# A gated-attention encoder layer: the residual x reaches the output projection by accumulating DMAs instead of plain loads

## The chip, the cores and the metric

The kernel runs on one core of a Trainium2 chip. The metric is the device time of one execution in microseconds (us), taken as the median of several runs. The profile shows one execution of the kernel before. Engines: PE is TensorE (PEld its weight load), DVE is VectorE, ACT is ScalarE, POOL is GpSimd, SP is SyncE, which only issues transfers.

## What is computed

One encoder layer on x of 1024 rows by 1024 columns. Two branches (gated linear attention, and windowed pooling) are projected and merged; what matters here is the end:

```python
DEEPNORM_ALPHA = (2.0 * DEPTH) ** 0.25          # DEPTH = 1
merged = g_a * (y_a @ w_proj_a) + g_b * (y_b @ w_proj_b)
y = merged @ w_out
return _layernorm(DEEPNORM_ALPHA * x + y, ln_g, ln_b)

def _layernorm(x, g, b):
    mu = jnp.mean(x32, axis=-1, keepdims=True)
    var = jnp.mean(jnp.square(x32 - mu), axis=-1, keepdims=True)
    return ((x32 - mu) * lax.rsqrt(var + EPS) * g + b).astype(x.dtype)
```

A layer norm does not change when its input and the root of its eps are both multiplied by one constant. So the norm of alpha·x + y with eps is the norm of x + y/alpha with eps/alpha².

## The kernel before

**Products.** A matrix product is done in blocks of two by two quarters, with seven block products in place of eight (`PRODUCTS`, called 1 to 7). Each is twelve matmuls of 128x128 by 128x512: four steps of k, each three times, since every operand is split into a high and a low part (`split`: ACT casts the high part, DVE subtracts it to get the low one). The weights of a product are the operands B11, B21, B22 and T1 to T4 (sums and differences of quarters), made by `Operands.make` in 128x1024 pieces; the rows' side is made by `prep` (DVE sums `raw…`) and `ring_split` (`whi`, `wlo`).

**The w_out stage.** Four objects `Pair` (o0 to o3, from `out_pair`) each give two row blocks of 128: pair tb gives rows tb and tb+4. Their products are interleaved for o0 and o1, then come o2 and o3. Each pair has PSUM banks by tag: `a` (products 1, 2), `c` (7, 4), `b` (6, with T2) and `d` (5, 3); a tag has two buffers (`bank`). Sums common to several quarters, `u` and `e`, are made from banks a, b, c.

**The residual.** `residual` allocates a row `z` and loads x into it on SP's queue (eight loads of 512 KB). `pre` then makes alpha·z + u (or e) on DVE, and `use` adds the product's bank. The first quarter, (0,0), is alpha·z + bank a.

**The norm.** For o0 to o2: after each half row ACT sums it (`junk_…s`, with tb, i, half in its name, written to a spare PSUM buffer of tags b and d in turn); after the fourth, `norm_pair` takes the mean (`nm`), ACT squares four half rows into spare PSUM buffers, DVE and POOL (a power) make the factor, `shifted` scales the row on ACT and multiplies by ln_g on DVE, and POOL issues an accumulating DMA that adds the row to `out`, where ln_b has been stored. For the last pair, o3, `bn_stats` and `norm_one` on DVE do it, and SP stores half rows.

**Order.** The program's order gives the priorities; a scheduler with its own timing then fixes the sequence of each engine. Each engine runs its instructions in that sequence, so an instruction that waits holds up all that stand behind it. In both kernels the end of PE's sequence is: o2's T2, o2's T1, o3's B11, o2's T4 and B22, o3's T3, B21, T2, T1, T4, B22 (twelve matmuls each, the B11 of o3 partly before T4).

Of the kernel before, what the change touches and what calls it, by code (L numbers as in the profile page):

```python
# [7 lines left out]
F32 = mybir.dt.float32  # L8
# [3 lines left out]
AF = mybir.ActivationFunctionType  # L12
ALU = mybir.AluOpType
# [3 lines left out]
P = 128  # L17
S = 1024
D = 1024
# [9 lines left out]
EPS = 1e-5  # L29
AHEAD = 3  # L30
LEAD = 4
ALPHA = 2.0 ** 0.25
# [4 lines left out]
def encoder_layer(ctx: ExitStack, tc: tile.TileContext, xT, x, w_av, w_v, w_blk, w_up, b_al, g_norm,  # L37
                  w_pool, p_scale, b_mrg, w_pa, w_pb, w_o, ln_g, ln_b, ident_c, rcnt_c, masks_c, out):
    nc = tc.nc
    act, dve, pool_e, pe, sp = nc.scalar, nc.vector, nc.gpsimd, nc.tensor, nc.sync  # L40
# [10 lines left out]
    def split(src, hi, lo, lo_eng=None):  # L51
        act.copy(hi, src)  # L52
        (lo_eng or dve).tensor_tensor(out=lo, in0=src, in1=hi.bitcast(F32), op=ALU.subtract)  # L53
# [129 lines left out]
    def at(q):  # L183
        return int(q[0]) - 1, int(q[1]) - 1

    class Operands:
        def __init__(self, nm, fetch):
            self.nm, self.fetch, self.ops, self.pool, self.td = nm, fetch, {}, {}, {}

        def ahead(self, g, piece, eng):  # L190

            q = {}
            for n in ("22", "12", "11", "21"):
                q[n] = piece(n, f"{self.nm}p{n}_{g}")
                self.fetch(q[n], n, g)
            for o, out_, a, b, op in (("T3", "22", "22", "12", ALU.subtract), ("T1", "12", "12", "11", ALU.subtract),
                                      ("T2", "11", "22", "11", ALU.add), ("T4", "21", "21", "11", ALU.subtract)):
                eng.tensor_tensor(out=q[out_], in0=q[a], in1=q[b], op=op)
                self.td[o, g] = dram.tile([P, 2, 512], F32, name=f"{self.nm}{o}_{g}d", tag=f"{self.nm}{o}_{g}d")
                sp.dma_start(self.td[o, g], q[out_])  # L200

        def make(self, o, pool):

            self.pool[o] = pool
            self.ops[o] = [pool.tile([P, 4, 512], F32R, tag="op", name=f"{self.nm}{o}{n}") for n in "hl"]
            for g in range(2):
                t = c4.tile([P, 2, 512], F32, tag="c", name=f"{self.nm}{o}_{g}")
                with tc.high_priority(offset=120):
                    if o[0] == "T":
                        sp.dma_start(t, self.td[o, g])  # L210
                    else:
                        self.fetch(t, o[1:], g)
                split(t, *(x[:, 2 * g:2 * g + 2, :] for x in self.ops[o]))

    X = Operands("x", lambda t, q, g: sp.dma_start(
        t, xT.rearrange("(k p) t -> p k t", p=P)[:, 4 * at(q)[0] + 2 * g:4 * at(q)[0] + 2 * g + 2, at(q)[1] * 512:at(q)[1] * 512 + 512]))
    WO = Operands("wo", lambda t, q, g: sp.dma_start(
        t, w_o[at(q)[1], 4 * at(q)[0] + 2 * g:4 * at(q)[0] + 2 * g + 2].rearrange("k p c -> p k c")))
    for q in ("11", "21", "22"):
        X.ops["B" + q] = [xq[n][at(q)[0]][at(q)[1]] for n in range(2)]  # L220
        X.pool["B" + q] = op_a
# [21 lines left out]
    for half in range(2):  # L243
        ps = ps_m.tile([P, 512], F32, tag="m", name=f"ps_at{half}")
# [204 lines left out]
            dve.tensor_copy(v[b][:, hs], po)  # L449
            act.activation(po, v[b][:, hs], AF.Square, accum_out=d["ss"][:, b:b + 1])  # L450

    def rsqrt_mean(ss, n, pool, nm, w, meanwhile=lambda: None):

        a = pool.tile([P, w], F32, tag="rs_a", name=f"rsa_{nm}", bufs=2)
        r = pool.tile([P, w], F32, tag="rs_r", name=f"rsr_{nm}", bufs=2)
        t = pool.tile([P, w], F32, tag="rs_t", name=f"rst_{nm}", bufs=2)
        dve.tensor_scalar(out=a, in0=ss, scalar1=1.0 / n, scalar2=EPS, op0=ALU.mult, op1=ALU.add)
        pool_e.tensor_tensor(out=r, in0=a, in1=mhalf[:, :w], op=ALU.pow)  # L458
        meanwhile()
        dve.tensor_tensor(out=t, in0=r, in1=r, op=ALU.mult)  # L460
        dve.tensor_tensor(out=t, in0=t, in1=a, op=ALU.mult)
        dve.tensor_scalar(out=t, in0=t, scalar1=-0.5, scalar2=1.5, op0=ALU.mult, op1=ALU.add)
        dve.tensor_tensor(out=r, in0=r, in1=t, op=ALU.mult)
        return r
# [115 lines left out]
    post = ctx.enter_context(tc.tile_pool(name="post", bufs=1, reuse_waits="tile"))  # L580
# [3 lines left out]
    hs_ = (slice(0, 512), slice(512, 1024))  # L584

    def row(nm):
        return c4.tile([P, S], F32, tag="c", name=nm)
# [209 lines left out]
    for gi in (0, 1, 3, 2):  # L797
        pair, p = pool_pair(gi)
# [17 lines left out]
    more = [ahead(YB, 0), None, ahead(YB, 1), None]  # L816
# [9 lines left out]
    more = [ahead(YA, 0), ahead(YA, 1), None, change(X, YB)]  # L826
# [51 lines left out]
    ln, z, st = {}, {}, {}  # L878
# [6 lines left out]

    def residual(tb):
        z[tb] = row(f"z_{tb}")
        with tc.high_priority(offset=150):
            sp.dma_start(z[tb], x[tb * P:tb * P + P, :])

# [7 lines left out]
    def small(nm, shape, tag, bufs=2):  # L898
        return post.tile([P] + shape, F32, tag=tag, name=nm, bufs=bufs)

    def shifted(t, r, nb):

        act.activation(z[t], z[t], AF.Identity, bias=nb, scale=r)
        for i in range(2):
            dve.tensor_tensor(out=z[t][:, hs_[i]], in0=z[t][:, hs_[i]], in1=ln["g"][i], op=ALU.mult)
        pool_e.dma_start(out[t * P:t * P + P, :], z[t], accum_op=ALU.add)

    def norm_pair(tb, sm):

        ln_rows()  # L910
        nm, ss = small(f"nm_{tb}", [2], "nm"), small(f"ss_{tb}", [2, 2], "ssq")
        dve.tensor_tensor(out=nm, in0=sm[:, :, 0], in1=sm[:, :, 1], op=ALU.add)
        for i in range(2):
            for half in range(2):
                junk = bank(f"junk_{tb}{i}{half}", next(spare))
                act.activation(junk, z[tb + 4 * i][:, hs_[half]], AF.Square, bias=nm[:, i:i + 1], accum_out=ss[:, i, half:half + 1])
        s2 = small(f"s2_{tb}", [2], "s2")
        dve.tensor_tensor(out=s2, in0=ss[:, :, 0], in1=ss[:, :, 1], op=ALU.add)
        r = rsqrt_mean(s2, D, post, f"ln{tb}", 2)
        nb = small(f"nb_{tb}", [2], "nb")  # L920
        dve.tensor_tensor(out=nb, in0=nm, in1=r, op=ALU.mult)
        for i in range(2):
            shifted(tb + 4 * i, r[:, i:i + 1], nb[:, i:i + 1])

    def norm_one(t, st):
        mv = small(f"mv_{t}", [2], "mv")
        dve.bn_aggr(out=mv, in_=st)
        zz = z[t]
        r = rsqrt_mean(mv[:, 1:2], 1, post, f"ln{t}", 1, meanwhile=lambda: [
            dve.scalar_tensor_tensor(out=zz[:, cs], in0=zz[:, cs], scalar=mv[:, 0:1], in1=ln["g"][i],  # L930
                                     op0=ALU.subtract, op1=ALU.mult) for i, cs in enumerate(hs_)])
        for i, cs in enumerate(hs_):
            dve.scalar_tensor_tensor(out=zz[:, cs], in0=zz[:, cs], scalar=r, in1=ln["b"][i], op0=ALU.mult, op1=ALU.add)
            sp.dma_start(out[t * P:t * P + P, cs], zz[:, cs])

    def out_pair(tb):
        end = tb == 3
        sm, st = [], {}

        def fetch(t, i, h):  # L940
            t = k4(t)
            if h == 0 or tb > 1:
                sp.dma_start(t, m_d[h][:, :, cols(tb, i)])
            else:
                for k in range(4):
                    dve.tensor_copy(t[:, k, :], m_last[4 + k][:, cols(tb, i)])

        def part(i, half):
            t = tb + 4 * i
            if t not in z:  # L950
                residual(t)
            return z[t][:, hs_[half]]

        def pre(i, half, more):
            o = part(i, half)
            dve.scalar_tensor_tensor(out=o, in0=o, scalar=ALPHA, in1=more, op0=ALU.mult, op1=ALU.add)

        def use(i, half, ps, more):
            o = part(i, half)
            if more is None:  # L960
                dve.scalar_tensor_tensor(out=o, in0=o, scalar=ALPHA, in1=ps, op0=ALU.mult, op1=ALU.add)
            else:
                dve.tensor_tensor(out=o, in0=ps, in1=o, op=ALU.add)
            if end:
                if i not in st:
                    st[i] = small(f"bst_{tb}{i}", [2, 6], "bst")
                dve.bn_stats(out=st[i][:, half, :], in_=o)
                if (i, half) == (1, 0):
                    norm_one(tb + 4, st[1])
            else:  # L970
                if not sm:
                    sm.append(small(f"sm_{tb}", [2, 2], "sm"))
                junk = bank(f"junk_{tb}{i}{half}s", next(spare))
                act.activation(junk, o, AF.Identity, scale=-1.0 / D, accum_out=sm[0][:, i, half:half + 1])

        def done():
            if end:
                norm_one(tb, st[0])
            else:
                norm_pair(tb, sm[0])  # L980

        return Pair(f"o{tb}", fetch, WO, use, done, late={"22": 1} if tb < 2 else None, pre=pre, order="1765423" if end else "1765243")

    outs = [out_pair(tb) for tb in range(4)]
    n = len(items) - 10
# [73 lines left out]
```

## Time and profile before

| | |
|---|---|
| median of 3 runs | 953.77 us (953.29 to 954.65) |
| the profiled execution | 952.35 us, span of the trace 950.6 us |
| mean granted clock of PE | 0.992 of full speed |
| busy share of the span | PE 97%, DVE 78%, ACT 42%, POOL 5% |
| w_out's products in the trace | about 849 us to 941 us; the rest of the span, 9.7 us, is the last norm |

The table says how full each engine is over the whole; the change touches only the last 100 us or so, and those are read in the rows further down.

### The profile page before, as it was taken

How to read it: one execution, taken by the hardware profiler on the slowest of the kernel's cores; microseconds unless marked ns; L12 is line 12 of the kernel's file. 1: busy time of each engine (PE TensorE's matmuls, PEld its weight loads, DVE VectorE, ACT ScalarE, POOL GpSimd, SP SyncE). 2: the span in 40 equal slices, each digit the busy share in tenths (PEclk: the TensorE clock that was granted, in tenths of full speed). 3: DMA queues.
4: the chain of work that ended last, by engine and by line, in shares of the span. 5: the costliest groups of instructions: out<-in, count | busy, mean ns of one | idle time of the engine just before them, and what ended most of it. 6: DMA issues, size and time to landing. Idle time of an engine off the chain costs nothing. (4 is left out here: it accounts for less than half of the span.)

```text
span 950.6 us, 13001 instructions
## 1 busy us (share of the span) xinstructions
PE 926.2 (97%) x4744; PEld 752.7 (79%) x4744; DVE 738.3 (78%) x1168; ACT 401.5 (42%) x676; POOL 43.0 (5%) x35
## 2 busy tenths in 40 slices
PE   9999999999999999999999999999999999997995
PEld 6887897987888887888878778888888878775873
DVE  5448969879768658868787788787787977799777
ACT  5156335354241326323333333346552533644661
POOL 1430000000010000000000000000000000000021
PEclk9999999999999999999999999999999999998998
DMA  8931112323316666162222289798696786769264
GB/s 270 362 115 35 59 57 58 95 73 86 114 51 206 220 198 242 65 249 92 69 75 70 90 309 356 242 365 294 210 344 198 271 292 211 232 204 354 63 128 93
DMA packets 84143, 169.13 MB, mean 178 GB/s; under 512 B 11456, under 2 KB 28096, under 8 KB 84080
## 3 DMA queue, kind: packets, MB, share of 16 engines
q1 hardware_dynamic: 83216, 165.16, 51.0%
q0 software_dynamic: 864, 3.15, 2.0%
q8 instruction: 37, 0.61, 0.3%
q14 instruction: 26, 0.21, 0.1%
HBM read 114.80 MB, written 53.48 MB: 177 GB/s over the span
## 5 line engine op out<-in xcount | busy, mean ns | idle before, releaser
L123 PE MATMUL ps_la<-xh,whi_la 128*128 128x512 f32 x128 | 51.6, 403 | 0.0
L123 PE MATMUL ps_la<-xl,whi_la 128*128 128x512 f32 x128 | 51.4, 402 | 0.0
L123 PE MATMUL ps_la<-xh,wlo_la 128*128 128x512 f32 x128 | 50.9, 398 | 0.0
L52 ACT CAST whi_gb<-raw_gb 128x512 fp32r<-128x512 f32 x28 | 17.3, 621 | 48.8 <-PE psd_pi L638 14.8
L141 PE MATMUL ps_v<-whi_v,xh 128*128 128x264 f32 x128 | 37.2, 292 | 0.2 <-DVE v L150 0.2
L141 PE MATMUL ps_v<-wlo_v,xh 128*128 128x264 f32 x128 | 37.2, 292 | 0.0
L141 PE MATMUL ps_v<-whi_v,xl 128*128 128x264 f32 x128 | 36.5, 286 | 0.0
L52 ACT CAST whi_lb<-raw_lb 128x512 fp32r<-128x512 f32 x28 | 17.4, 621 | 36.9 <-PE psd_lb L638 9.1
L52 ACT CAST whi_pi<-raw_pi 128x512 fp32r<-128x512 f32 x28 | 17.4, 620 | 32.8 <-PE psd_gb L638 7.1
L52 ACT CAST whi_gta<-raw_gta 128x512 fp32r<-128x512 f32 x28 | 17.3, 618 | 32.4 <-DVE raw_gta L623 7.3
L52 ACT CAST whi_pb<-raw_pb 128x512 fp32r<-128x512 f32 x28 | 17.1, 619 | 32.7 <-PE psd_pb L638 11.2
L458 POOL TENSOR_TENSOR rsr_ln<-rsa_ln,mhalf 128x2 f32<-128x2 f32 (+1 forms) x5 | 4.6, 924 | 581.0 <-PE psc_o L638 569.1
L123 PEld LDWEIGHTS ps_la<-xh,wlo_la 128*128 128x128 f32 x128 | 24.1, 188 | 5.7 <-issue 0.4
L123 PEld LDWEIGHTS ps_la<-xh,whi_la 128*128 128x128 f32 x128 | 24.1, 188 | 5.4
L123 PEld LDWEIGHTS ps_la<-xl,whi_la 128*128 128x128 f32 x128 | 24.1, 188 | 5.3
L389 ACT ACTIVATE e<-e 128x1024 f32<-128x1024 f32 x20 | 21.0, 1058 | 17.1 <-DVE e L388 17.1
L449 DVE COPY v<-ps_o 128x256 f32<-128x256 f32 x32 | 13.5, 423 | 18.4 <-PE ps_o L446 11.3
L52 ACT CAST whi_o<-raw_o 128x512 fp32r<-128x512 f32 x28 | 16.9, 616 | 24.6 <-DVE raw_o L623 8.8
L53 DVE TENSOR_TENSOR wlo_pi<-raw_pi,whi_pi 128x512 fp32r<-128x512 f32 x28 | 19.2, 686 | 10.3 <-ACT whi_pi L52 10.0
L450 ACT ACTIVATE ps_o<-v 128x256 f32<-128x256 f32 x32 | 12.4, 388 | 32.6 <-DVE v L449 32.6
L392 DVE TENSOR_TENSOR qs<-q,e 128x1024 f32<-128x1024 f32 x20 | 24.3, 1214 | 2.3 <-ACT e L389 1.5
L123 PE MATMUL ps_k<-xh,whi_k 128*128 128x512 f32 x64 | 25.8, 402 | 0.0
(586 smaller groups left out, 3043.5 us busy)
## 6 DMA issues: line engine op xcount, KB each, us to landing
raw_v<-in_w_v SPq DMA_DIRECT2D x16, 264.0 KB, 2.6
xp<-in_xT SPq DMA_DIRECT2D x8, 512.0 KB, 6.6
oT<-oTs SPq DMA_DIRECT2D x32, 128.0 KB, 2.6
raw_la<-in_w_blk SPq DMA_DIRECT2D x8, 512.0 KB, 3.4
wop<-in_w_o SPq DMA_DIRECT2D x8, 512.0 KB, 4.6
la<-la SPq DMA_DIRECT2D x8, 512.0 KB, 3.1
raw_pi<-in_w_blk SPq DMA_DIRECT2D x16, 256.0 KB, 4.1
raw_gb<-in_w_blk SPq DMA_DIRECT2D x16, 256.0 KB, 2.7
```

The lines of the kernel that those rows point to most:

```text
L52: act.copy(hi, src)
L53: (lo_eng or dve).tensor_tensor(out=lo, in0=src, in1=hi.bitcast(F32), op=ALU.subtract)
L123: pe.matmul(ps[:, half * 512:half * 512 + 512], lhsT=a, rhs=mov(b, k, half), start=(i == 0), stop=(i == 23))
L141: pe.matmul(o, lhsT=sta(a, k, tb), rhs=w(k - k0)[b], start=(k == 0 and i == 0), stop=(k == KB - 1 and i == 2))
L389: act.activation(e, e, AF.Exp, scale=1.0 / TAU)
L392: dve.tensor_tensor(out=qs, in0=qt[h], in1=e, op=ALU.mult)
L449: dve.tensor_copy(v[b][:, hs], po)
L450: act.activation(po, v[b][:, hs], AF.Square, accum_out=d["ss"][:, b:b + 1])
L458: pool_e.tensor_tensor(out=r, in0=a, in1=mhalf[:, :w], op=ALU.pow)
```

## The change

Four things change. First, the rows of o0, o1 and o2 are no longer loaded: `use` writes the product's bank plus u or e to the half row of z (ACT copies bank a for the first quarter, DVE adds for the others), and then POOL issues a DMA that adds 256 KB of x to that half row in SBUF: twelve such DMAs; six loads of 512 KB leave SP's queue, two (for o3) stay. `pre` is left for o3 alone. Second, 1/alpha goes into w_out's operands as they are made (`act.mul` in place of the cast, a scalar_tensor_tensor in place of the subtraction) and 1/alpha² into eps, so that z is x + y/alpha. Third, `shifted` scales in two halves. Fourth, through these the scheduler orders the engines anew.

```diff
     class Operands:
-        def __init__(self, nm, fetch):
+        def __init__(self, nm, fetch, scale=None):
+            self.scale = scale
...
-                split(t, *(x[:, 2 * g:2 * g + 2, :] for x in self.ops[o]))
+                hi, lo = (x[:, 2 * g:2 * g + 2, :] for x in self.ops[o])
+                if self.scale is None:
+                    split(t, hi, lo)
+                else:
+                    act.mul(hi, t, self.scale)
+                    dve.scalar_tensor_tensor(out=lo, in0=t, scalar=self.scale, in1=hi.bitcast(F32), op0=ALU.mult, op1=ALU.subtract)
...
     def residual(tb):
         z[tb] = row(f"z_{tb}")
+        if tb % 4 < 3:
+            return
         with tc.high_priority(offset=150):
             sp.dma_start(z[tb], x[tb * P:tb * P + P, :])
...
     def shifted(t, r, nb):
-        act.activation(z[t], z[t], AF.Identity, bias=nb, scale=r)
         for i in range(2):
+            act.activation(z[t][:, hs_[i]], z[t][:, hs_[i]], AF.Identity, bias=nb, scale=r)
             dve.tensor_tensor(out=z[t][:, hs_[i]], in0=z[t][:, hs_[i]], in1=ln["g"][i], op=ALU.mult)
...
-        r = rsqrt_mean(s2, D, post, f"ln{tb}", 2)
+        r = rsqrt_mean(s2, D, post, f"ln{tb}", 2, EPS / ALPHA ** 2)
...
         def pre(i, half, more):
             o = part(i, half)
-            dve.scalar_tensor_tensor(out=o, in0=o, scalar=ALPHA, in1=more, op0=ALU.mult, op1=ALU.add)
+            dve.tensor_tensor(out=o, in0=o, in1=more, op=ALU.add)
 
         def use(i, half, ps, more):
             o = part(i, half)
-            if more is None:
-                dve.scalar_tensor_tensor(out=o, in0=o, scalar=ALPHA, in1=ps, op0=ALU.mult, op1=ALU.add)
+            if end:
+                dve.tensor_tensor(out=o, in0=ps, in1=o, op=ALU.add)
             else:
-                dve.tensor_tensor(out=o, in0=ps, in1=o, op=ALU.add)
+                if more is None:
+                    act.copy(o, ps)
+                else:
+                    dve.tensor_tensor(out=o, in0=ps, in1=more, op=ALU.add)
+                t = tb + 4 * i
+                pool_e.dma_start(o, x[t * P:t * P + P, hs_[half]], accum_op=ALU.add)
...
-        return Pair(f"o{tb}", fetch, WO, use, done, late={"22": 1} if tb < 2 else None, pre=pre, order="1765243" if ...)
+        return Pair(f"o{tb}", fetch, WO, use, done, late={"22": 1} if tb < 2 else None, pre=pre if end else None, order=...)
```

Three places of the new order follow. In the names, `whi_6_o0` is the high part for product 6 of pair o0, `z_4` is row block 4.

**Start of w_out, ACT.** ACT's sequence where the last pieces of operand B21 are made and the products with T2 (product 6 of o0 and o1) get ready. Before:

```order
L52 CAST woB21h_7397<-woB21_0_7399 128x1024
L52 CAST woB21h_7397<-woB21_1_7403 128x1024
L52 CAST woT4h_7456<-woT4_0_7458 128x1024
L52 CAST whi_6_o0_7557<-raw11_o0_7306 128x512
L52 CAST woT4h_7456<-woT4_1_7462 128x1024
L52 CAST whi_6_o1_7582<-raw11_o1_7344 128x512
```

ACT's sequence at the same place after the change:

```order
L218 ACTIVATE woB21h_7397<-woB21_0_7399 128x1024
L218 ACTIVATE woB21h_7397<-woB21_1_7403 128x1024
L52 CAST whi_6_o0_7557<-raw11_o0_7306 128x512
L218 ACTIVATE woT4h_7456<-woT4_0_7458 128x1024
L52 CAST whi_6_o1_7582<-raw11_o1_7344 128x512
L52 CAST whi_5_o0_7600<-raw21_o0_7370 128x512
```

The cast for product 6 of o0 now stands ahead of the first piece of T4. On DVE, the four sums `raw…` that these casts read stood behind the second piece of `woB21l`, and now stand ahead of it.

**Middle of w_out, ACT.** ACT's sequence around the operand of product 2 of o2. Before:

```order
L974 ACTIVATE junk_110s_7798,sm_1_7713<-z_5_7665 128x512
L916 ACTIVATE junk_000_7831,ss_0_7829<-z_0_7642,nm_0_7828 128x512
L52 CAST whi_2_o2_7936<-raw12_o2_7779 128x512
L643 COPY u_o2_7932<-psa_o2_7919 128x512
L916 ACTIVATE junk_010_7835,ss_0_7829<-z_4_7638,nm_0_7828 128x512
```

And ACT's sequence there after the change, from the sum over the last half row of o0:

```order
L987 ACTIVATE junk_001s_7815,sm_0_7678<-z_0_7724 128x512
L924 ACTIVATE junk_000_7828,ss_0_7826<-z_0_7724,nm_0_7825 128x512
L924 ACTIVATE junk_001_7830,ss_0_7826<-z_0_7724,nm_0_7825 128x512
L924 ACTIVATE junk_010_7832,ss_0_7826<-z_4_7675,nm_0_7825 128x512
L924 ACTIVATE junk_011_7834,ss_0_7826<-z_4_7675,nm_0_7825 128x512
L52 CAST whi_2_o2_7938<-raw12_o2_7774 128x512
L649 COPY u_o2_7934<-psa_o2_7921 128x512
```

The cast `whi_2_o2` now stands behind that sum, which waits for the accumulating DMA of the half row, and behind all four squares of o0.

**End of w_out, POOL.** POOL's whole sequence from the norm of o0 to the last row that it adds to `out`. Before:

```order
L906 DMA out_0<-z_0_7642 128x1024
L906 DMA out_0<-z_4_7638 128x1024
L906 DMA out_0<-z_1_7669 128x1024
L906 DMA out_0<-z_5_7665 128x1024
L458 TENSOR_TENSOR rsr_ln2_8079<-rsa_ln2_8078,mhalf_82 128x2
L906 DMA out_0<-z_2_7979 128x1024
L906 DMA out_0<-z_6_7975 128x1024
```

POOL's sequence there after the change (`z_2` and `z_6` are the rows of o2):

```order
L914 DMA out_0<-z_0_7724 128x1024
L976 DMA z_2_8017<-in_x 128x512
L914 DMA out_0<-z_4_7675 128x1024
L976 DMA z_6_7995<-in_x 128x512 x2
L914 DMA out_0<-z_1_7748 128x1024
L914 DMA out_0<-z_5_7700 128x1024
L976 DMA z_2_8017<-in_x 128x512
L464 TENSOR_TENSOR rsr_ln2_8080<-rsa_ln2_8079,mhalf_82 128x2
L914 DMA out_0<-z_2_8017 128x1024
```

The four half rows of o2 are interleaved with the four rows of o0 and o1 that go out, and the last half row stands behind all four. On DVE at the end, the two multiplications by ln_g of row z_6 and the two L938 of row z_7 stood ahead of the last add (`z_3` with bank d) before, and stand behind it now.

## Rows read from the trace of the kernel before

**Rows 1.** The page, busy time, share and instructions of each engine.

```profile
PE 926.2 (97%) x4744; PEld 752.7 (79%) x4744; DVE 738.3 (78%) x1168; ACT 401.5 (42%) x676; POOL 43.0 (5%) x35
```

**Rows 2.** Windows of 20 us: busy time and count by engine, granted clock, DMA share, GB/s.

```profile
860.00:880.00 20.00, 13.77 (x53) 10.62 (x53) 17.98 (x27) 9.52 (x13) 0.00 (x0) 0.83 0.97 364
880.00:900.00 20.00, 20.00 (x88) 16.24 (x87) 14.43 (x25) 11.06 (x28) 0.00 (x0) 1.00 0.24 69
```

**Rows 3.** Timeline of PE: start, duration, what, idle time before and its releaser.

```profile
866.05 0.80 PE L638 MATMUL psb_o<-woT2h,whi_o 128*128 128x512 f32 x1 [5.98 <-ACT whi_o L52]
...
907.07 0.40 PE L638 MATMUL psd_o<-woT1h,whi_o 128*128 128x512 f32 x1
907.30 0.40 PE L638 MATMUL psd_o<-woT1l,whi_o 128*128 128x512 f32 x1
...
922.48 0.50 PE L638 MATMUL psa_o<-woB21h,whi_o 128*128 128x512 f32 x1 [1.30 <-ACT whi_o L52]
...
924.55 0.63 PE L638 MATMUL psa_o<-woB21h,wlo_o 128*128 128x512 f32 x1
924.98 0.63 PE L638 MATMUL psa_o<-woB21h,whi_o 128*128 128x512 f32 x1
...
927.54 0.50 PE L638 MATMUL psb_o<-woT2h,whi_o 128*128 128x512 f32 x1
...
937.66 0.47 PE L638 MATMUL psd_o<-woB22h,whi_o 128*128 128x512 f32 x1 [1.48 <-DVE z L963]
...
940.30 0.40 PE L638 MATMUL psd_o<-woB22h,wlo_o 128*128 128x512 f32 x1
```

**Rows 4.** Timeline of ACT, 861 to 866 us.

```profile
861.85 1.04 ACT L52 CAST woB21h<-woB 128x1024 fp32r<-128x1024 f32 x1 [2.51 <-DMA woB<-in_w_o]
864.43 1.04 ACT L52 CAST woT4h<-woT 128x1024 fp32r<-128x1024 f32 x1 [1.54 <-DMA woT<-woT_0d]
865.38 0.61 ACT L52 CAST whi_o<-raw_o 128x512 fp32r<-128x512 f32 x1
```

**Rows 5.** Timeline of DVE, 862 to 867 us.

```profile
862.92 1.22 DVE L53 TENSOR_TENSOR woB21l<-woB,woB21h 128x1024 fp32r<-128x1024 f32 x1 [2.02 <-ACT woB21h L52]
864.07 2.49 DVE L623 TENSOR_TENSOR raw_o<-raw_o,raw_o 128x512 f32<-128x512 f32 x4
```

**Rows 6.** DMA issues, 850 to 951 us: count, KB each, median us to landing.

```profile
out<-z SPq DMA_DIRECT2D x4, 256.0 KB, 2.0
```

**Rows 7.** Timeline of POOL, 919 to 934 us: issues of accumulating rows.

```profile
919.87 0.86 POOL L906 DMA_DIRECT2D out<-z  x1 [6.13 <-ACT junk_210s L974]
921.66 0.86 POOL L906 DMA_DIRECT2D out<-z  x1 [0.94 <-ACT whi_o L52]
...
933.08 0.90 POOL L906 DMA_DIRECT2D out<-z  x1 [5.91 <-DVE z L905]
```

**Rows 8.** Landings of POOL's rows: those issued at 919.87 and 921.66, then at 933.08.

```profile
DMA to landing us min/median/max: 6.8/7.2/7.5
...
DMA to landing us min/median/max: 5.3/5.3/5.3
```

**Rows 9.** Window holding the last two accumulating rows, columns as in rows 2.

```profile
933.00:943.00 10.00, 6.23 (x26) 4.36 (x24) 9.87 (x24) 0.00 (x0) 2.95 (x4) 1.00 0.65 105
```

**Rows 10.** The page's DMA queues: packets, MB, share of 16 engines over the span.

```profile
q1 hardware_dynamic: 83216, 165.16, 51.0%
q0 software_dynamic: 864, 3.15, 2.0%
```

**Rows 11.** Groups by form, 870 to 951 us: busy us, mean ns, idle before.

```profile
L916 ACT ACTIVATE junk<-z,nm 128x512 f32<-128x512 f32 x12 | 8.1, 677 | 0.6 <-DVE nm L912 0.6
L905 DVE TENSOR_TENSOR z<-z,lng 128x512 f32<-128x512 f32 x12 | 7.7, 687 | 0.7 <-ACT z L903 0.7
```

**Rows 12.** Timeline of DVE at the end.

```profile
939.51 1.40 DVE L930 SCALAR_TENSOR_TENSOR z<-z,mv,lng 128x512 f32<-128x512 f32 x2
...
940.91 0.68 DVE L963 TENSOR_TENSOR z<-psd_o,z 128x512 f32<-128x512 f32 x1
```

More of the change, by code (lines that the diff above doesn't have):

```diff
@@ L217, in encoder_layer @@
     WO = Operands("wo", lambda t, q, g: sp.dma_start(
-        t, w_o[at(q)[1], 4 * at(q)[0] + 2 * g:4 * at(q)[0] + 2 * g + 2].rearrange("k p c -> p k c")))
+        t, w_o[at(q)[1], 4 * at(q)[0] + 2 * g:4 * at(q)[0] + 2 * g + 2].rearrange("k p c -> p k c")), 1.0 / ALPHA)
     for q in ("11", "21", "22"):
@@ L450, in outputs, with rsqrt_mean @@
             act.activation(po, v[b][:, hs], AF.Square, accum_out=d["ss"][:, b:b + 1])
-    def rsqrt_mean(ss, n, pool, nm, w, meanwhile=lambda: None):
+    def rsqrt_mean(ss, n, pool, nm, w, eps=EPS, meanwhile=lambda: None):
         a = pool.tile([P, w], F32, tag="rs_a", name=f"rsa_{nm}", bufs=2)
@@ L456, in rsqrt_mean @@
         t = pool.tile([P, w], F32, tag="rs_t", name=f"rst_{nm}", bufs=2)
-        dve.tensor_scalar(out=a, in0=ss, scalar1=1.0 / n, scalar2=EPS, op0=ALU.mult, op1=ALU.add)
+        dve.tensor_scalar(out=a, in0=ss, scalar1=1.0 / n, scalar2=eps, op0=ALU.mult, op1=ALU.add)
         pool_e.tensor_tensor(out=r, in0=a, in1=mhalf[:, :w], op=ALU.pow)
@@ L928, in norm_one @@
         zz = z[t]
-        r = rsqrt_mean(mv[:, 1:2], 1, post, f"ln{t}", 1, meanwhile=lambda: [
+        r = rsqrt_mean(mv[:, 1:2], 1, post, f"ln{t}", 1, EPS / ALPHA ** 2, meanwhile=lambda: [
             dve.scalar_tensor_tensor(out=zz[:, cs], in0=zz[:, cs], scalar=mv[:, 0:1], in1=ln["g"][i],
@@ L980, in done @@
                 norm_pair(tb, sm[0])
-        return Pair(f"o{tb}", fetch, WO, use, done, late={"22": 1} if tb < 2 else None, pre=pre, order="1765423" if end else "1765243")
+        return Pair(f"o{tb}", fetch, WO, use, done, late={"22": 1} if tb < 2 else None, pre=pre if end else None, order="1765423" if end else "1765243")
     outs = [out_pair(tb) for tb in range(4)]
```

## The prediction

> **What bounds the kernel now.** I read the page first: PE is busy 97% of the span [rows 1], so a change can only win where PE waits, and DVE passes that vanish while PE runs are worth nothing. The windows show where PE waits in w_out's stage. From 860 to 880 us it is busy 13.77 of 20, at a mean granted clock of 0.83 and with the DMA engines at 0.97; from 880 to 900 it is full while DVE is busy 14.43 of 20 [rows 2]. PE's timeline then gives every wait that matters: 5.98 us before the first T2 product, which waits for ACT's cast `whi`; 1.30 before o3's B21; 1.48 before the last product, where a PSUM bank waits for DVE's add; 940.7 is where PE ends [rows 3]. Matmuls follow each other 0.23 us apart at full clock (907.07 to 907.30) and 0.43 apart after a wait, while the clock is at its lower level (924.55 to 924.98) [rows 3]. So twelve matmuls are 2.8 us, and the dozen after a long wait costs up to some 2 us more.
>
> The whole forecast therefore has five terms: four PE waits that shrink, appear or move, and the tail after the last matmul.
>
> **a) The first wait, 5.98 us.** Now: ACT's second half of `woB21h` ends at 862.89, then ACT waits for the T4 piece until 864.43, casts it, and only then, at 865.38, makes `whi` for product 6 [rows 4]. DVE meanwhile makes `woB21l` from 862.92 and the four sums from 864.07 [rows 5]. After the change the sums stand ahead of `woB21l` and the cast stands right behind `woB21h`: it starts at about 862.9 instead of 865.38, so PE starts 2.5 us earlier. Bounds: 3.5 if the loads of B21 and T4 also land earlier, now that four 512 KB loads of x no longer stand beside them; 0.5 if they land later, since B21's last load stands two transfers further back on SP. **−2.5.**
>
> The other small edits cost nothing here: the scaled cast and the scaled subtraction take the places of passes of the same size on the same engines, and the nine DVE passes of `pre` that vanish lie in stretches where PE is full [rows 2]. Scaling in half rows adds six ACT instructions off the path; the loads that leave SP are only felt in a).
>
> **What an accumulating half row costs.** No row of before has x added to SBUF. The nearest are POOL's six rows into `out`, 512 KB each. They hold the 16 DMA engines 2.0% of 950.6 us [rows 10], which is 19 us, or 3.2 us each; the only two in 933 to 943 us say the same, 0.65 of 10 us [rows 9]. One that starts on an empty queue lands 5.3 us after issue [rows 7, 8], so about 2.1 us are fixed. Two issued 1.8 us apart, at 919.87 and 921.66, landed after 6.8 and 7.5 us [rows 7, 8], so 2.5 us apart: they pass one behind the other on POOL's queue. I take 3.0 for a row when rows queue (bounds 2.5 and 3.25). For a half row the lower bound is a plain transfer of 256 KB, by SP's queue 0.51 x 950.6 us for 165.16 MB [rows 10], 0.77 us; the upper is a whole row, 3.25, if the count of packets and not the bytes sets the time. I take half a row, 1.5, and 2.1 fixed behind it.
>
> The Trainium skill, page "DMA: Bandwidth & Descriptors", section "Anatomy of one DMA — SWDGE (gpsimd) path", fits a transfer issued from GpSimd as about 2.0 us plus its bytes over 436 KB per us. By that a whole row would land in 3.2 us and a half row in 2.6; the trace's 5.3 disagrees for rows that accumulate, though the fixed part agrees.
>
> **b) A new wait before o2's product 2.** PE runs o0's last product, o1's, o2's B11 and T3, then o2's B21. From the end of o0's last product that leaves 36 matmuls, 8.4 us. ACT's cast for B21 now stands behind the sum of o0's last half row and four squares. So after that product come: the add, 0.7 (a DVE pass of 128x512, 0.69 [rows 11]); the half row, 2.1 + 1.5; the sum, 0.8; small steps, 0.3; four squares of 0.7 (0.677 and the gap [rows 11]), 2.8; the cast, 0.6 [rows 4]. That is 8.8, plus about 1 because the half row of o1 before it is still on the queue: 9.8, 1.4 late. Bounds 0.4 (plain rate) and 2.6 (whole-row price). **+1.4.**
>
> **c) The wait before o3's T2.** This is the largest term. T2 of o3 writes bank `b`, and that buffer is held by a square of o2 (`junk_200`), which needs o2's mean, which needs the sum of o2's last half row, `junk_201s`, which now waits for the landing of POOL's last half row. On POOL's queue that transfer stands behind four rows of `out` and three half rows. Before, from the end of o2's T2 (907.07) to o3's T2 (927.54) took 20.5 us [rows 3], for 72 matmuls that need 16.7 (the rest are waits at 922.48 and the lower clock behind them).
>
> After: the first of the rows goes out once its last multiplication is done, which on DVE stands right behind `u`, two passes or 1.35 us after T2's end. Then the queue must pass four rows (4 x 3.0), four half rows (4 x 1.5) and, on the same DMA engines, the two loads that remain for o3 (2 x 1.54 by SP's rate [rows 10]): 21.1. The fixed part is 2.1. Then sum, mean and one square, 0.8 + 0.2 + 0.9 = 1.9. Together 26.5, against 20.5: **+6.0.** Bounds with rows at 2.5 and half rows at 0.77: +1.0; with rows at 3.25 and half rows at 1.6: +7.4.
>
> A check from the other side: POOL issues two of these rows shortly ahead of the last half row. Were nothing else queued, it would still land 2 x 3.0 + 1.5 + 2.1 = 9.6 us after issue, and PE has only T3 and B21, 5.6 us, less the add and 1.9.
>
> **d) From o3's T2 to PE's end.** 13.2 us now (927.54 to 940.7), with the 1.48 wait [rows 3]. That wait goes, since two multiplications by ln_g and a `pre` no longer stand ahead of the add on DVE. But after a wait of 6 us or more the clock falls, as it did for the eight matmuls behind the first wait, which is 8 x 0.2 = 1.6, or 1.7 with the start. **+0.2**, bounds −1.5 and +2.
>
> **e) The tail.** 9.7 us from PE's end to the span's end, DVE busy throughout. Two L930 (1.40 together) lie just ahead of the last add, at 939.51, and the add at 940.91 [rows 12]; they and two multiplications by ln_g of 0.69 [rows 11] now stand behind it. That is 2.6, less about 0.5 that covers waits for POOL's powers: **+2.1**, bounds 1.3 and 2.6. Cover gone, it is the 2.6.
>
> **Sum.** −2.5 + 1.4 + 6.0 + 0.2 + 2.1 = +7.2. The profiled execution took 952.35 us, so 959.55; the median of the runs is 1.42 above it (953.77), which gives **961.0 us**. The five bounds added up give −2.3 and +14.1 (951.5 to 967.9), the likeliest case's own range.
>
> **Rivals.** A measurement of this kernel tells 0.2%, 1.9 us, from no change: 951.9 and 955.7 are the borders.
>
> *B, half rows are cheap and quick: faster.* If a half row lands like SP's plain store of 256 KB, 2.0 us after issue [rows 6], and does not stand behind the rows for `out`, T2 of o3 finds its bank free. From the end of o2's last product to o3's T2 there are 24 matmuls, 5.6 us; less the add (0.7) and 1.9, a landing within 3.0 us means no wait at all. Then c) is 16.7 − 20.5 = −3.8, d) −1.5, b) 0.4, a) and e) as above: −5.3, or 948.5. It decides from a landing of about 8 us downward, where c) is +1.5 and the sum zero. Against it: rows do queue [rows 8], and one alone took 5.3. The skill's fit above points this way. 0.15.
>
> *C, a half row costs as much as a whole one: slower still.* With 3.25, c) is 1.35 + 12 + 13 + 3.1 + 2.1 + 1.9 − 20.5 = +13.0, and b) 2.6: +15.4, or 969.2. For it: six rows left 864 packets [rows 10], 144 each, and a half row covers as many partitions. Against it: nothing here shows cost by count. 0.12.
>
> *D, gains and losses cancel: the change does nothing.* Half rows at 0.77 and rows at 2.8 make c) +2.3; with b) 0.6, a) −3.0, d) −0.8, e) 1.8 the sum is +0.9, or 954.7. It needs every unknown at its kind end. 0.13.
>
> **How the numbers follow.** The main case has 0.60 and its time is the forecast. Faster is B with a little of the main case's low end, 0.16; same is most of D, 0.13; slower is the rest, 0.71. The range leaves out B and the upper half of C: 952 to 969.
>
> **What would show it.** a): the wait before the first T2 product falls to about 3.5 us. b): a wait of 1 to 2 us before o2's B21, released by ACT. c): a wait of 5 to 10 us before o3's T2, released by a square of o2, with ACT idle before `junk_201s` on a DMA of z, and that half row landing 10 to 14 us after issue; a landing under 8 would make the prediction wrong. d): no wait before the last B22, and a lower clock in the first dozen matmuls of T2. e): 11 to 12 us from PE's last matmul to the span's end. Half rows that land 3 to 4 us after issue on an empty queue speak for 1.5, over 5 for C.

## The result

The changed kernel takes **963.64 us** (median of 4 runs, 959.5 to 968.45); the kernel before took 954.18 us (4 runs, 953.29 to 954.65) beside it. The ratio is 1.0112, with a 95% interval of 1.0091 to 1.0132. (The medians alone give 1.0099.) It is slower, as forecast; the forecast was 961.0 us, in a range of 952 to 969.

The profiled execution took 959.5 us, the shortest of the four; its span is 957.7 us. The page gives the busy time of each engine and the two DMA queues of this kernel, which answer to [rows 1] and [rows 10]:

```profile
PE 927.5 (97%) x4744; PEld 754.3 (79%) x4744; DVE 729.8 (76%) x1156; ACT 405.2 (42%) x685; POOL 52.6 (5%) x47
...
q1 hardware_dynamic: 82352, 162.02, 50.3%
q0 software_dynamic: 2592, 6.29, 3.9%
```

PE has done the same work; it waited longer. The software queue moved 6.29 MB in 3.9% of 957.7 us, 37.4 us of all 16 engines. The six rows for `out` are 19 of that [rows 10], so the twelve half rows took 18.3 us, **1.5 us each**, as taken in the forecast. They left 2592 − 864 = 1728 packets, 144 each, as many as a row, so the count of packets does not set the time here; rival C (a half row at the price of a row) is out.

These are PE's waits in w_out's stage after the change (timeline, columns as in [rows 3]), with the first matmul of the stage and the last:

```profile
845.12 0.40 PE L644 MATMUL psa_o<-woB11h,whi_o 128*128 128x512 f32 x1
...
860.60 0.50 PE L644 MATMUL psb_o<-woT2h,whi_o 128*128 128x512 f32 x1 [4.19 <-ACT whi_o L52]
...
862.51 0.79 PE L644 MATMUL psb_o<-woT2h,whi_o 128*128 128x512 f32 x1 [0.98 <-ACT whi_o L52]
...
900.36 0.49 PE L644 MATMUL psa_o<-woB21h,whi_o 128*128 128x512 f32 x1 [2.27 <-ACT u_o L649]
...
903.19 0.40 PE L644 MATMUL psb_o<-woT2h,whi_o 128*128 128x512 f32 x1
...
924.36 0.80 PE L644 MATMUL psa_o<-woB21h,whi_o 128*128 128x512 f32 x1 [4.32 <-ACT whi_o L52]
...
931.92 0.50 PE L644 MATMUL psb_o<-woT2h,whi_o 128*128 128x512 f32 x1 [2.31 <-ACT junk L924]
...
944.45 0.39 PE L644 MATMUL psd_o<-woB22h,wlo_o 128*128 128x512 f32 x1
```

The first wait has shrunk from 5.98 us [rows 3] to 4.19; the one two matmuls later is 0.98. Two waits are new: 2.27 before o2's B21, which ends with ACT's copy `u`, and 2.31 before o3's T2, ended by a square (`junk`). The wait before o3's B21 has grown from 1.30 to 4.32. The chain of work that ended last shows what stands behind the last of them:

```profile
920.38 0.60 POOL out L914
920.98 9.04 DMA z<-in_x
...
930.11 0.73 ACT junk_201s L987 x2
...
931.06 0.82 ACT junk L924 x2
...
931.92 4.61 PE psb_o L644 x12
```

POOL issues a row for `out` at 920.38, then o2's last half row at 920.98; that takes 9.04 us to land, then follow the sum on ACT, the mean on DVE, one square, and T2 starts. POOL's timeline shows what that half row stood behind:

```profile
907.79 0.91 POOL L914 DMA_DIRECT2D out<-z  x1 [2.20 <-DVE rst_ln L467]
909.06 0.88 POOL L976 DMA_DIRECT2D z<-in_x  x1 [0.35 <-ACT z L972]
909.73 1.11 POOL L914 DMA_DIRECT2D out<-z  x1
911.53 0.88 POOL L976 DMA_DIRECT2D z<-in_x  x1 [0.69 <-DVE rsr_ln L469]
913.24 0.87 POOL L976 DMA_DIRECT2D z<-in_x  x1 [0.84 <-DVE z L974]
918.96 0.87 POOL L914 DMA_DIRECT2D out<-z  x1 [4.85 <-DVE z L913]
920.38 0.87 POOL L914 DMA_DIRECT2D out<-z  x1 [0.54 <-DVE z L913]
920.98 1.18 POOL L976 DMA_DIRECT2D z<-in_x  x1
```

The `out` rows (L914) and the half rows (L976) are interleaved from 907.79 on. The eight half rows of o0 and o1, issued from 877 to 894 us, had no row ahead of them. The view of the tile z on POOL gives the landing of the last three (issued from 888 to 900 us), and then that of the first (877.28):

```profile
DMA to landing us min/median/max: 3.7/3.8/4.1
...
DMA to landing us min/median/max: 5.0/5.0/5.0
```

The three are near the 3.6 (2.1 fixed and 1.5) of the forecast; beside them SP moved nothing. The first had nothing ahead of it on POOL's queue, but SP was loading `raw_o` beside it. Those between them, close behind one another, took up to 6.6.

To compare kernels I cut the stage at matmuls that all of them have, each time from the start of the one to the start of the other in PE's timeline: A from o0's first B11 to the first T2; B to o2's T3; C to o2's T2; D to o3's T2; E to the last matmul; F from there to the span's end.

| kernel (one profiled execution each) | A | B | C | D | E | F | sum |
|---|---|---|---|---|---|---|---|
| before | 17.27 | 32.70 | 5.51 | 23.28 | 12.76 | 10.30 | 101.8 |
| changed | 15.48 | 34.55 | 8.04 | 28.73 | 12.53 | 13.25 | 112.6 |

So the stage became 10.8 us longer. The span grew by 7.1 only, since w_out began 3.7 us earlier in this execution (845.12 against 848.78). The traces below show that start between 845.1 and 850.6; two of them (the rows on SP, and o1's rows behind) run the same PE sequence in w_out as the changed kernel and begin at 849.6 and 848.8, and a second profile of the changed kernel (run 6) begins at 846.7. I therefore read the change by the stage and by medians, not by the one span.

### The profile page after: what moved, and what is told of

It reads as the page before. It is cut to its first block, busy times and chain, and to the rows that moved or that the text cites. A ratio compares the mean times of both kernels' runs of the same rounds, so it can differ in the third digit from the quotient of the medians.

```text
span 957.7 us, 13009 instructions
## 1 busy us (share of the span) xinstructions
PE 927.5 (97%) x4744; PEld 754.3 (79%) x4744; DVE 729.8 (76%) x1156; ACT 405.2 (42%) x685; POOL 52.6 (5%) x47
## 3 DMA queue, kind: packets, MB, share of 16 engines
q1 hardware_dynamic: 82352, 162.02, 50.3%
q0 software_dynamic: 2592, 6.29, 3.9%
## 4 chain that ended last, share of the span: by engine, by line
PE 88%; DVE 5%; DMA 3%; issue 2%; ACT 1%; POOL 0%; DVEq 0%; SPq 0%; POOLq 0%; ACTq 0%
PE ps_v L141 10%; PE ps_la L123 9%; PE ps_k L123 5%; PE ps_q L123 5%; PE psc_lb L644 2%; PE psd_gb L644 2%; PE psd_pb L644 2%; PE psd_gta L644 2%; PE psc_pb L644 2%; PE psa_pb L644 2%; PE psa_gb L644 2%; PE psa_pi L644 2%; PE psa_lb L644 2%; PE psd_lb L644 2%; PE psa_gta L644 2%; PE psc_gb L644 2%
## 5 line engine op out<-in xcount | busy, mean ns | idle before, releaser
L976 POOL DMA_DIRECT2D z<-in_x x12 | 11.0, 943 | 557.6 <-DMA raw_o<-m 547.8
L52 ACT CAST whi_pb<-raw_pb 128x512 fp32r<-128x512 f32 x28 | 17.1, 619 | 32.5 <-PE psd_pb L644 11.2
L53 DVE TENSOR_TENSOR wlo_o<-raw_o,whi_o 128x512 fp32r<-128x512 f32 x28 | 19.0, 689 | 9.6 <-ACT whi_o L52 9.3
```

Of the source, the lines that this page charges most:

```text
L976: pool_e.dma_start(o, x[t * P:t * P + P, hs_[half]], accum_op=ALU.add)
```

## The experiments

Theory Q: the loss is made by accumulating half rows whose landing something on PE's path waits for. Rival R: the folding, the half rows and the new order make it. Further rivals stand with the runs. In the diffs a minus is the changed kernel unless another is named. Ratios are to the kernel before, timed beside each.

**1. No accumulating DMA.** The loads by SP and the adds on DVE come back; the folding and the scaling in half rows stay.

```diff
-        if tb % 4 < 3:
-            return
...
-            if end:
+            if True:
                 dve.tensor_tensor(out=o, in0=ps, in1=o, op=ALU.add)
...
-pre=pre if end else None
+pre=pre
```

> The changed kernel without the accumulating DMAs of x: all eight rows of x are loaded by SP and added on DVE as before; 1/alpha in w_out's operands and the scaling in half rows stay. Theory Q (the loss is made by the half rows on POOL's queue): all waits on a landing of z go, 949 to 954 us, no slower than before. Rival R (the folding, the half rows of the scaling and the new order make the loss): 958 to 965 us.

Measured: 951.62 us, ratio 0.9976 (0.9962 to 0.9990). The accumulating DMAs, with the order that the scheduler makes for them, are the whole loss, and what is left of the change gains a little. Of rival R the folding and the half rows of the scaling are out. The new order is not parted from the DMAs here: without them the scheduler orders the engines anew, and PE's sequence in w_out differs too. Runs 3, 4, 5 and 9 look at that.

**2. o2's rows by loads.** As run 1, for o2 alone (`tb % 4 < 2`, `if tb > 1`, `pre if tb > 1`).

> The changed kernel, but o2's two rows are loaded by SP and added on DVE; o0 and o1 keep their eight accumulating DMAs. Theory Q: the waits before o3's B21 and T2 (4.3 and 2.3 us) go and the tail is short again, the wait before o2's B21 (2.3 us) stays: 951 to 956 us. Rival R: 958 to 965 us. If the cost lies with o0's and o1's half rows instead: 957 to 961.

Measured: 957.39 us, ratio 1.0040 (1.0027 to 1.0053). The tail F is 11.2 and D 22.2, so what o2's half rows cost is gone. But the total is 1.4 us above what Q gave and inside the range of the last rival, and C is 11.84: o0's and o1's half rows cost far more than in the forecast's b). PE's timeline shows the wait:

```profile
905.72 0.79 PE L644 MATMUL psa_o<-woB21h,whi_o 128*128 128x512 f32 x1 [3.61 <-ACT u_o L649]
```

The windows in and behind it, columns as in [rows 2]:

```profile
902.00:905.00 3.00, 0.11 (x1) 0.00 (x0) 0.25 (x2) 3.00 (x9) 0.00 (x0) 0.99 0.01 3
...
906.00:908.00 2.00, 2.00 (x5) 1.54 (x6) 1.78 (x8) 1.95 (x6) 0.00 (x0) 0.50 0.01 4
908.00:910.00 2.00, 2.00 (x6) 1.59 (x5) 0.00 (x0) 2.00 (x7) 0.00 (x0) 0.50 0.00 0
```

The wait is 3.61 us here, and the clock is at its lower level for the dozen matmuls behind it. In the changed kernel's profile it stayed at full speed behind 2.27 us.

**3. Rows for `out` as plain stores on SP** (this leaves out the addition of ln_b to six rows).

```diff
-        pool_e.dma_start(out[t * P:t * P + P, :], z[t], accum_op=ALU.add)
+        sp.dma_start(out[t * P:t * P + P, :], z[t])
```

> The changed kernel, but the rows of o0, o1 and o2 go out as plain stores on SP's queue; this leaves out the addition of ln_b to these six rows. POOL's queue then holds the twelve half rows alone. Theory Q: o2's last half row lands 3.5 to 5 us after issue instead of 9.0, the waits before o3's B21 and T2 shrink to 0 to 2.5 us together: 950 to 956 us. Rival L (the landing of a half row even on an empty queue, 3.7 us and its follow-up on ACT, makes the loss): 957 to 962 us.

Measured: 958.41 us, ratio 1.0050 (1.0032 to 1.0069). By the total rival L has it; the stage divides it. D falls from 28.7 to 22.7, below that of before: the waits before o3's B21 and T2 are 1.25 and 1.26, as theory Q has it. What remains lies in C (9.85, with the lower clock) and F (12.6), and C is rival L at another place: o0's last half row, with no row ahead of it on POOL's queue, landed 4.2 us after issue, and ACT's sum, squares, cast and copy follow it up to o2's B21:

```profile
898.76 0.60 ACT L987 ACTIVATE junk_001s<-z 128x512 f32<-128x512 f32 x1 [0.66 <-DMA z<-in_x]
```

The last half row of o2 lands 5.7 us after issue, longer than I gave it; beside it SP moved a load for o3 and two of the six rows.

**4. o1's rows behind o2's last half row.** All the work stays.

```diff
+                    r, nb = rows[0]
+                    dve.scalar_tensor_tensor(out=nb, in0=o[:, 0:2], scalar=0.0, in1=nb, op0=ALU.mult, op1=ALU.add)
                 pool_e.dma_start(o, x[t * P:t * P + P, hs_[half]], accum_op=ALU.add)
+                if behind:
+                    for a in range(2):
+                        shifted(1 + 4 * a, r[:, a:a + 1], nb[:, a:a + 1])
```

> The changed kernel with one small DVE instruction that makes the scaling of o1's rows wait for the add of o2's last half row (it adds zero times two elements of that half row to the factor nb), so that on POOL's queue o1's two rows stand behind o2's last half row. All the work stays. Theory Q: that half row lands 4 to 6 us after issue, the waits before o3's B21 and T2 are 0 to 3 us together, the tail is short again: 951 to 956 us. Rival L: 957 to 962 us. Rival R: no change, 958 to 965.

Measured: 962.94 us, ratio 1.0105 (1.0076 to 1.0134): a miss in the total. The number is the one that rival R gave for no change, but the kernel did change. The last half row does land sooner, after 6.1 us, no wait is left before o3's T2, and F is 10.85 again. But the wait moved to o3's B21 and grew, in PE's timeline:

```profile
932.50 0.79 PE L644 MATMUL psa_o<-woB21h,whi_o 128*128 128x512 f32 x1 [7.85 <-ACT whi_o L52]
```

ACT's timeline ahead of that:

```profile
927.87 0.60 ACT L997 ACTIVATE junk_210s<-z 128x512 f32<-128x512 f32 x1 [1.46 <-DMA z<-in_x]
...
928.50 0.60 ACT L52 CAST whi_o<-raw_o 128x512 fp32r<-128x512 f32 x1
929.01 2.92 ACT L912 ACTIVATE z<-z,nb,rsr_ln 128x512 f32<-128x512 f32 x4
931.84 0.60 ACT L52 CAST whi_o<-raw_o 128x512 fp32r<-128x512 f32 x1
```

ACT waits for another half row, `junk_210s`, which landed 10 us after issue behind o0's rows, then runs four scalings that now stand there, and only then casts the operand of B21 (931.84). So the place in POOL's queue is one part of the cause; the place in ACT's sequence is another.

**5. o0's squares behind the cast and copy for o2's B21**, on top of run 2.

```diff
         dve.tensor_tensor(out=nm, in0=sm[:, :, 0], in1=sm[:, :, 1], op=ALU.add)
+        if tb == 0:
+            dve.scalar_tensor_tensor(out=nm, in0=outs[2].u[:, 0:2], scalar=0.0, in1=nm, op0=ALU.mult, op1=ALU.add)
...
+    outs[2].hooks = {0: [lambda: norm_pair(0, held[0])]}
```

> The kernel of the run with o2's rows by loads, and besides one small DVE instruction that makes the mean of o0 wait for the copy of o2's u (it adds zero times two elements of u): on ACT the cast and the copy that o2's B21 waits for then stand ahead of o0's four squares, behind o0's last sum as before. Theory S (o0's and o1's half rows cost through ACT's order before o2's B21, wait and lower clock after it): that wait falls from 3.6 to 0 to 0.8 us, o2's T3 to T2 from 11.8 to 5.5 to 6.5 us, total 951 to 953.5 us. Rival P (the cost is elsewhere, in the transfers themselves or POOL): 956 to 958 us.

Measured: 955.04 us, ratio 1.0023 (1.0007 to 1.0039), between the two. The wait before B21 fell as theory S has it, and a new one came up one product later:

```profile
900.25 0.50 PE L644 MATMUL psa_o<-woB21h,whi_o 128*128 128x512 f32 x1 [0.36 <-ACT u_o L649]
...
905.48 0.50 PE L644 MATMUL psb_o<-woT2h,whi_o 128*128 128x512 f32 x1 [2.21 <-ACT junk L926]
```

o2's T2 waits 2.21 us for a square: the PSUM buffer of tag b that it needs is the spare buffer of a square of o0. This is the same kind of hold as before o3's T2 in the changed kernel. It comes with this run's edit: the first four squares start at 901.27, before the instruction that holds back o0's mean has run (901.34 to 901.50), so they are o1's, and o0's stand behind them.

**6. The changed kernel again.**

> The changed kernel once more. Its runs spread over 9 us where those of before spread over 1.4. Theory K (a wait of 2 to 4 us before o2's B21 and o3's products sometimes brings the lower clock and sometimes not, as the execution falls): the same waits as in the first profile within 1 us, but the dozen matmuls of o2's B21 at the lower clock, o2's T3 to T2 10 us instead of 8.0; runs 959 to 969 us. Rival M (the landings differ between executions): waits before o2's B21 or o3's B21 and T2 that are longer by 2 us or more at the same clock.

Measured: 961.20 us (959.89 to 963.95), ratio 1.0085 (1.0058 to 1.0113). Neither theory is borne out: segments A to F are 15.3, 34.6, 8.0, 28.7, 12.5 and 13.0, each within 0.3 us of the first profile, waits and clock alike. The four runs spread over 4 us this time, and the kernel before over 950.53 to 955.82 in its 24 runs here, so the 9 us of the first four did not come back. No profile shows an execution like that of 968.45 us; what made it long is not shown.

**7 and 8. The folding alone, and the half rows alone**, each on the kernel before (run 7 is run 1 with the scaling in whole rows).

> The kernel before with 1/alpha folded into w_out's operands and eps alone; x by SP's loads, scaling in whole rows. The first wait shrinks by 1.5 to 2 us and the lower clock takes it back. Theory F (the folding gives what the run without accumulating DMAs won): 951 to 953 us. If the half rows of the scaling gave it: 953.5 to 954.5.

> The kernel before with the scaling in half rows alone. Theory F: 953.5 to 954.5 us, no difference. If the half rows of the scaling gave what the run without accumulating DMAs won: 951 to 953.

Measured: 950.61 us for the folding, ratio 0.9978 (0.9962 to 0.9994); 952.54 us for the half rows, 0.9992 (0.9979 to 1.0006). By the ratios theory F holds. The times themselves lie 0.4 and 1.0 us below its two ranges, since the kernel before, timed beside them, took 952.59 us here and 954.03 beside run 1. The folding alone, with or without the half rows (run 1), is ahead of both kernels. Its gain is not in A and B (49.0 against 50.0) by as much as the shorter first wait would give; D is 1.2 shorter and E 0.7 (the last wait of PE is 0.91 instead of 1.48).

**9. The squares in SBUF**, with all twelve accumulating DMAs. The sums stay in PSUM.

```diff
-                junk = bank(f"junk_{tb}{i}{half}", next(spare))
+                junk = post.tile([P, 512], BF16, tag="junk", name=f"junk_{tb}{i}{half}", bufs=1)
```

> The changed kernel, but the squares of the norm (not the sums) are written to a small SBUF tile in bfloat16 instead of spare PSUM buffers; what they add up is the same. Theory B (o3's T2 waits since a square holds its PSUM buffer until o2's last half row has landed): no wait before o3's T2 that a square ends, o2's T2 to o3's T2 25 to 27 us instead of 28.7, the wait before o3's B21 stays at 3.5 to 5 us, total 2 to 5 us less than the changed kernel, 956.5 to 959.5 us. Rival (T2 is late by its operand or by ACT's queue anyhow): the same wait with another releaser, total 960 to 963.

Measured: 954.43 us, ratio 1.0007 (0.9992 to 1.0022): no loss is left that this can tell, and the gain is about twice what I expected. Only one wait of PE still goes back to the landing of a half row, 1.46 us before o3's T1, whose cast stands behind `junk_200s` on ACT, though the landings are as long as ever. PE's timeline has these waits from 900 us on:

```profile
925.04 0.50 PE L644 MATMUL psd_o<-woT1h,whi_o 128*128 128x512 f32 x1 [1.46 <-ACT whi_o L52]
...
935.28 0.47 PE L644 MATMUL psd_o<-woB22h,whi_o 128*128 128x512 f32 x1 [1.00 <-DVE rsa_ln L463]
```

The second follows a plain load: ahead of the add that this product waits for, DVE waits for a row of o3, which SP loads, in DVE's timeline:

```profile
933.05 0.69 DVE L964 TENSOR_TENSOR z<-z,u_o 128x512 f32<-128x512 f32 x1 [1.28 <-DMA z<-in_x]
```

Of o2's half rows the last two, issued at 915.58 and 918.28, landed as follows, in the view of the tile z:

```profile
DMA to landing us min/median/max: 9.2/9.9/10.6
```

With the buffers free the scheduler also puts T2 ahead of B21 in o2 and o3, which gives ACT more time for B21's cast. Buffer and order changed together here; this run does not part them. C to F together are 54.3 against 62.6 in the changed kernel, 51.9 in the kernel before and 50.3 in run 1: against the folding without accumulating DMAs some 4 us of the stage are still lost.

**10. Both**, run 9 with run 5's order.

> As the run with squares in SBUF, and besides o0's mean waits for the copy of o2's u, so that the cast and the copy for o2's B21 stand ahead of o0's squares. All twelve accumulating DMAs stay. Theories B and S together: o2's T3 to T2 5.5 to 6.5 us instead of 8.0, o2's T2 to o3's T2 25 to 27, total 954 to 957.5 us: the waits on landings of o2 that remain on ACT still cost 2 to 4 us against before. If the transfers themselves cost time elsewhere: 958 or more.

Measured: 954.87 us, ratio 1.0014 (0.9999 to 1.0028), as expected in the total, but no better than run 9: there was no wait before o2's B21 left to take.

**11. Folding and squares in SBUF**, without accumulating DMAs.

> The kernel before with 1/alpha folded in and the squares written to a small SBUF tile in bfloat16; x by SP's loads, no accumulating DMA of x. Looks for a version ahead of both kernels. If the spare PSUM buffers cost the kernel before something too, as its waits of 1.3 and 1.5 us would allow: 947.5 to 950 us. If they only hurt where a landing of z stands behind them: 950 to 952, as with the folding alone.

Measured: 956.80 us, ratio 1.0026 (1.0008 to 1.0044): slower than the folding alone, a miss. In its profile the last product waits 3.55 us for DVE, and DVE had waited for o3's rows:

```profile
929.47 0.69 DVE L962 TENSOR_TENSOR z<-z,u_o 128x512 f32<-128x512 f32 x1 [4.74 <-DMA z<-in_x]
...
932.30 0.69 DVE L962 TENSOR_TENSOR z<-z,u_o 128x512 f32<-128x512 f32 x1 [2.14 <-DMA z<-in_x]
```

SP's loads of these rows wait until a row of `out` has left. Here they are issued at 921.5 and 924.3 and land after 7.8 and 7.9 us; with the folding alone (run 7) they are issued at 914.4 and 917.1 and land after 3.9. Why o0's rows leave later in this order is not shown. C to F together are 54.5, as in run 9 with its twelve accumulating DMAs (54.3), but through other waits, so this run does not say what the accumulating DMAs cost in run 9.

The stages of the runs that the reading rests on, cut as above:

| run | A | B | C | D | E | F | sum |
|---|---|---|---|---|---|---|---|
| 1 no accumulating DMA | 15.66 | 34.55 | 5.51 | 21.81 | 12.04 | 10.93 | 100.5 |
| 2 o2 by loads | 15.20 | 33.54 | 11.84 | 22.16 | 12.04 | 11.20 | 106.0 |
| 3 rows on SP | 15.19 | 33.53 | 9.85 | 22.69 | 10.97 | 12.61 | 104.8 |
| 4 o1's rows behind | 15.25 | 33.60 | 10.11 | 29.87 | 11.89 | 10.85 | 111.6 |
| 5 o0's squares behind | 15.14 | 34.35 | 8.53 | 23.23 | 12.04 | 11.25 | 104.5 |
| 7 folding alone | 15.20 | 33.77 | 5.56 | 22.12 | 12.04 | 11.05 | 99.7 |

## Why the prediction was right, and where its steps were off

The direction, the mechanism and nearly the size were right. The profiled execution's 959.5 us against a sum of 959.55 is partly luck: the stage's terms came to +10.8 instead of +7.2, and its early start took 3.7 back. By medians the change costs 9.5 us and, in the second set of runs, 8.6, against the 7.2 of the sum.

*a) The first wait, −2.5.* The wait did shrink, A by 1.8, for the reason given: the cast follows `woB21h`, whose last piece came 0.8 us later in the stage than before (13.86 us behind the first matmul against 13.07), which the bounds allowed for. But B grew by 1.85, and the net is nothing, outside the bounds of −3.5 to −0.5. The step that failed is to book a shorter wait as a gain and leave out what follows it. Of the 1.85, 0.74 is the second wait, 0.98 now and 0.24 in the kernel before, in PE's timeline:

```profile
867.51 0.80 PE L638 MATMUL psb_o<-woT2h,whi_o 128*128 128x512 f32 x1 [0.24 <-ACT whi_o L52]
```

The rest, about 1.1, goes with the clock. Windows of the changed kernel behind the first wait, columns as in [rows 2]:

```profile
863.00:865.00 2.00, 2.00 (x6) 1.52 (x6) 2.00 (x4) 2.00 (x3) 0.00 (x0) 0.50 1.04 401
865.00:867.00 2.00, 2.00 (x7) 1.52 (x6) 2.00 (x3) 0.40 (x1) 0.00 (x0) 0.50 0.46 173
867.00:868.00 1.00, 1.00 (x4) 0.79 (x3) 1.00 (x2) 0.00 (x0) 0.00 (x0) 0.61 0.79 226
```

PE runs at the lower level until after 867 us, and now more matmuls fall into that stretch: 13 in the two windows from 863 to 867. It is back at full speed 7 us behind the first T2 (860.60); in the kernel before it was back 4 us behind it (866.05), in this window:

```profile
870.00:871.00 1.00, 1.00 (x6) 0.80 (x5) 1.00 (x3) 0.13 (x1) 0.00 (x0) 1.00 1.04 420
```

In run 1, without any accumulating DMA, B is 34.55 too; with the folding alone it is 33.77, and A and B together are 1.0 shorter than before.

*b) Before o2's B21, +1.4.* Right in place and cause, too small: C grew by 2.5, just inside the bound of 2.6. (By the sum's own terms that bound would be near 3.2, with a half row at 3.25 in place of 1.5.) ACT's timeline of the changed kernel has the sum, the squares and what waits behind them:

```profile
895.44 0.60 ACT L987 ACTIVATE junk_001s<-z 128x512 f32<-128x512 f32 x1 [0.88 <-DMA z<-in_x]
...
896.39 0.69 ACT L924 ACTIVATE junk<-z,nm 128x512 f32<-128x512 f32 x1 [0.23 <-DVE nm L920]
...
898.52 0.67 ACT L924 ACTIVATE junk<-z,nm 128x512 f32<-128x512 f32 x1
...
899.23 0.60 ACT L52 CAST whi_o<-raw_o 128x512 fp32r<-128x512 f32 x1
899.74 0.57 ACT L649 COPY u_o<-psa_o 128x512 f32<-128x512 f32 x1
```

The sum starts when the half row has landed, the four squares run to 899.2, then come the cast and, which the sum of the step left out, the copy of `u`: it reads the bank that B21 writes. From the end of o0's last product (889.76) to B21 it took 10.6 us against 9.8 in the sum; 0.5 of that is the copy. Run 5 takes this wait away; the hold of o2's T2 that it brings is not there in the changed kernel. Runs 2 to 4, with a wait of 2.5 to 3.6 us, also paid for a lower clock.

*c) Before o3's T2, +6.0.* D grew by 5.45, and along the path of the sum: from the issue of the first row (907.79) to the last landing (930.02) it took 22.2 us, against 23.2 for queue and fixed part, and from there to T2 the 1.9. The last half row landed 9.0 us after issue, just below the 10 to 14 I gave. The wait that I put before T2 came as two, 4.32 before B21 and 2.31 before T2, since ACT's cast for B21 stands behind `junk_210s`, another half row of o2:

```profile
922.55 0.60 ACT L987 ACTIVATE junk_210s<-z 128x512 f32<-128x512 f32 x1 [0.56 <-DMA z<-in_x]
...
923.18 1.12 ACT L52 CAST whi_o<-raw_o 128x512 fp32r<-128x512 f32 x2
930.11 0.60 ACT L987 ACTIVATE junk_201s<-z 128x512 f32<-128x512 f32 x1 [5.80 <-DMA z<-in_x]
```

Run 3 shows the queue's part (D 22.7 with the rows elsewhere), run 4 ACT's part. Run 9 shows landings of 9 to 11 us with one wait of 1.46 us left behind them, in another order and with other buffers.

The rule of the Trainium skill, page "DMA: Bandwidth & Descriptors", section "Anatomy of one DMA — SWDGE (gpsimd) path", gives an estimate of 2.6 us for 256 KB. The three half rows with neither a row ahead nor SP's loads beside them took 3.7 to 4.1, so the measurement differs for a DMA that accumulates, though less than for the rows.

*d) To PE's end, +0.2.* Measured −0.2. The last wait is gone, and a stretch at the lower clock follows the wait before T2, as forecast.

*e) The tail, +2.1.* Measured +2.95 (2.7 in run 6), above the bound of 2.6. It is the two L938 and two L913 behind the last add, in DVE's timeline, which answers to [rows 12]:

```profile
944.88 0.69 DVE L969 TENSOR_TENSOR z<-psd_o,z 128x512 f32<-128x512 f32 x1
...
945.54 1.41 DVE L938 SCALAR_TENSOR_TENSOR z<-z,mv,lng 128x512 f32<-128x512 f32 x2
946.86 1.29 DVE L913 TENSOR_TENSOR z<-z,lng 128x512 f32<-128x512 f32 x2
```

They take 2.6 us together without the waits that I had let cover a part; the other 0.35 is not traced. Runs 2 and 4, where o2's norm ends sooner, have a short tail again (11.2 and 10.85, with 10.9 in run 1).

Rivals B, C and D did not come about: a half row does not land in 2 us, does not cost a row, and the gains did not cancel the losses.

What stays open: why w_out's start differs by 4.4 us between executions with one order of PE there (by 1.6 between the two of the changed kernel itself), how much of it the change moves, and why the clock fell behind a wait of 2.46 us (run 3) and of 2.21 (o2's T2 in run 5) but not behind 2.27 and 2.18 (o2's B21 in the two profiles of the changed kernel). Nor is it shown what run 9 owes to the buffers and what to the order.

## What to carry to other kernels

When a load is replaced by an accumulating DMA, its landing moves from ahead of the products to behind them, so follow what waits for it: the queue it is issued on, every instruction that stands behind its reader on an in-order engine, and the buffers that the reader's scratch output holds. Here twelve transfers of 1.5 us each cost some 9 us against the kernel before through those. Scratch output outside the products' buffers, with the order that the scheduler then made, took the kernel back to the time of before, though not to that of the folding alone. Before booking a shorter PE wait as a gain, look at the next wait and at the clock in the stretch behind it.

## What the runs showed of the hardware

Accumulating DMAs cost the DMA engines by bytes in the two sizes seen here: 1.5 us for 256 KB into SBUF and 3.2 for 512 KB into `out`, at 144 packets each. The same half row took 3.7 to 4.1 us to land with no row ahead of it and SP idle, and up to 10.7 behind others (runs 9 and 10). Beside SP's transfers it took longer too: 5.0 us beside its loads, with nothing ahead on POOL's queue, and 5.7 beside a load and two stores in run 3, with no row on POOL's queue.
